# Layer 0 of a two-layer decoder: later places in the code for three loads, another order of the query products, another weave

## The chip, the cores and the metric

The kernel runs on one core of a Trainium2 chip. Its engines are TensorE (PE for its matmuls, PEld for its weight loads), VectorE (DVE), ScalarE (ACT), GpSimd (POOL) and SyncE (SP). SP issues most DMAs and computes nothing; POOL issues DMAs as well as computing. The metric is the device time of one execution in microseconds (us), lower is better; a kernel's time is the median of its runs.

## The reference

Two layers over 1024 tokens of width 1024, in float32. Cut to the part that the change touches, layer 0:

```python
def even_mixer(h, ...):                      # layer 0
    z = h @ w_in                             # qa, ka, va | cq | ckv | kr
    # A: sliding-window attention, 8 heads, window 128, rotary on qa and ka
    # B: latent attention, 8 heads: rms_norm(cq) @ w_uq -> q_nope, q_rope (rotary)
    #    rms_norm(ckv) @ w_ukv -> k_nope, v;  kr -> k_rope (rotary, shared)
    return concat(oa, ob) @ w_out

for layer in (0, 1):
    x = x + mixer[layer](rms_norm(x, mix_norm))
    x = x + memory_cross_attention(rms_norm(x, x_norm), rms_norm(mem, mem_norm), w_q, w_kv, w_o)
    x = x + swiglu(rms_norm(x, ffn_norm), w_gate, w_up, w_down)
return rms_norm(x, final_norm)
```

The memory (`mem`, 256 tokens) doesn't depend on x, so the keys and values that both layers make of it can be computed at any time.

## The kernel before, in words

**Products.** Each float32 operand is split into a high part h (rounded to the type fp32r) and a low part l, and a product is three matmuls: hh, hl, lh. A weight tile of 128 x 1024 comes by a DMA of 512 KB from SP into a raw tile `wr`, ACT copies it to `wh` (L213), and POOL subtracts in four pieces of 256 columns for `wl` (L182 by way of L217).

**Two lines of work.** The 1024 tokens are done in two halves of 512. A *sparse* line (tiles and matmuls named s) runs the attentions, norms and what follows them for one half, and a *dense* line (named d) runs projections for the other half and, later, the feed-forward net. `g_weave` (L297) runs both as generators: a step of the sparse line yields its size n in matmuls of 512 columns, and then the dense line is advanced by n times a ratio; a `Gap(n)` in the sparse line advances the dense line by n of these units. The ratios of the four mixed stretches are R0 to R4 and RA (L44); RA holds for `g_rest(0, 0)`, the last part of the first stretch. Steps of products in `g_rest` count only 0.05 (`DENSE`).

**Order.** The place in the code is a priority. At build time a scheduler puts each engine's instructions into one fixed order from it, out of code order where an operand or a tile isn't ready by its own reckoning. On the chip each engine, and each DMA queue, goes through its list in order and waits at whatever isn't ready. Tiles come from pools with a fixed number of buffers, given out in code order: the dense line has two raw tiles, three weight slots (a slot is a `wh` and a `wl`) and three PSUM banks; the pool of 16 KB tiles (`B16`, by `big`) has six, the pool `A4` four, and the pool of gain vectors `G` has one, which both lines share.

**The dense line of the first stretch** (`dense`, L1769) does, in this order: `proj0_units(0)`, the projections of layer 0 for the first half, with the read of the second half's tokens (`xB`, `squares_unit`) ahead of the last two units; then four key units and four value units of the memory for layer 0 (`memory_units(0)`, m0), with the norm of the second half (`norm_unit`) between the key units; the read of the first half's tokens `xA` (L1776); the load of the rotary tables `tabB` for the second half (L1780 to L1784, four DMAs at L520 that repeat rows for all partitions); the output projection `out_units` for the heads that are done; `proj0_units(1)`; and `memory_units(1)` (m1), the memory for layer 1. In `proj0_units` the last units are the queries `q_nope(0)`, `q_nope(4)` and then `q_rope`; the latent attention of the sparse line starts when all are marked done (`mark("mla", hf)`).

**The sparse line of the first stretch** (`sparse`, L1792): sliding-window attention `g_swa(0)`, latent attention `g_mla(0)`, then `g_rest(0, 0)`: the last part of the output projection, a norm (`x_norm`), the cross-attention to the memory, and a norm (`ffn_norm`). `g_norm_T` (L408) scales a block of 128 tokens on DVE (L420), has PE turn it (L403) and evacuates it by ACT and DVE; it yields a first `Gap` of N1 or N2 (8 and 15) and a `Gap` of 8 after each block. `factors` and `rstd` (L357) make a block's factor by some dozen DVE instructions on one column.

Queries go through DRAM: `q_rope`'s outcome is stored to `qrd` from the POOL queue (`to_rope`), and `g_mla` loads it from there into `qr` (L1396 to L1399).

Of the kernel before, what the change touches and what calls it, by code (L numbers as in the profile page):

```python
# [9 lines left out]
F32 = mybir.dt.float32  # L10
# [8 lines left out]
P = 128  # L19
S = 1024  # L20
D = 1024
# [17 lines left out]
N1, N2 = 8, 15  # L39
# [1 line left out]
START = ((0, 1), (1, 3))  # L41
PSS = 5
NSC = 2
R0, R1, RA, R2, R3, R4 = 2.6, 1.6, 2.3, 1.6, 2.3, 2.1  # L44


def host_constants():
# [61 lines left out]
class Ring:  # L109
# [3 lines left out]
    def next(self):  # L113
        self.i += 1
        return self.items[(self.i - 1) % len(self.items)]
# [47 lines left out]
class Builder:  # L163
# [430 lines left out]
    def memory_units(self, l, s):  # L594
        nc, I = self.nc, self.I
        ma = []

        xn = []

        def load():  # L600
            for b in range(2):
                xn.append(self.A4.tile([P, D], F32, tag="a4", name="mxn"))
                nc.sync.dma_start(xn[b], I["mem"][0, b * P:(b + 1) * P, :])
            return self.gain(f"l{l}_mem_norm")

        def prep(g):
            if l == 0:
                ss = self.st.tile([P, 4], F32, tag="ss", name="ss")
                for i in range(4):
                    nc.scalar.activation(self.t2(), xn[i // 2][:, i % 2 * 512:i % 2 * 512 + 512], AF.Square,  # L610
                                         accum_out=ss[:, i:i + 1])
                nc.vector.tensor_add(ss[:, 0:2], ss.rearrange("p (b h) -> p h b", h=2)[:, 0],
                                     ss.rearrange("p (b h) -> p h b", h=2)[:, 1])
                nc.vector.tensor_copy(self.rmem, self.rstd(ss[:, 0:2], 2, D))
            for b in range(2):
                nc.vector.scalar_tensor_tensor(xn[b], xn[b], self.rmem[:, b:b + 1], g, op0=ALU.mult, op1=ALU.mult)
            return iter(())

        def norm(_):
            m = self.big("mem")  # L620
            mv = [t.rearrange("p (k t) -> p k t", t=MEM) for t in (m[:, 0:2048], m[:, 2048:4096])]
            ma[:] = [(mv[0][:, k], mv[1][:, k]) for k in range(8)]
            for b in range(2):
                yield from self.g_turn(s if l else self.S, xn[b], lambda k0: tuple(t[:, k0:k0 + 4, b * P:(b + 1) * P] for t in mv))

        w = I[f"l{l}_w_xkv"]
        mkv = self.mkv[l]

        def save(ps, c):
            h, lo = self.a4()  # L630
            n = ps.shape[-1]
            self.split_ps(h[:, :n], lo[:, :n], ps)

            def put():
                self.move(mkv[:, c:c + n], h[:, :n])
                self.move(mkv[:, c + 1024:c + 1024 + n], lo[:, :n])

            self.later(put)

        pss = []  # L640

        def key(h):
            def f(wt):
                ps = s.ps()[:, :MEM]
                yield from self.g_projA(ps, wt, ma)
                save(ps, h * MEM)
            return lambda: self.wcols(s, w, h * P), f

        def value(k):
            def f(wt):  # L650
                if k == 0:
                    pss[:] = [s.ps() for _ in range(2)]
                for b in range(2):
                    c = slice(b * P, (b + 1) * P)
                    for j in range(2):
                        ah, al = ma[k + j]
                        for i, (a, x) in enumerate(((ah, wt[0]), (ah, wt[1]), (al, wt[0]))):
                            nc.tensor.matmul(pss[b], a[:, c], x[:, j], start=(k + j + i == 0),
                                             stop=(k + j == 7 and i == 2))
                        yield 3  # L660
                if k == 6:
                    for b in range(2):
                        save(pss[b], 2048 + b * 512)
            return lambda: self.wcols(s, w, 512, 512, k, 2), f

        yield load, prep
        yield (lambda: None), norm
        for h in range(4):
            yield key(h)
        for k in range(0, 8, 2):  # L670
            yield value(k)
        yield self.mark("mem", l)
# [267 lines left out]
    def g_rest(self, l, hf, x, xsrc, out, c0=0):  # L940

        nc, I, st, s = self.nc, self.I, self.st, self.S
        ts = slice(hf * 512, (hf + 1) * 512)
        if x is None:
            x = self.xtile("x")
# [2 lines left out]
                    nc.gpsimd.dma_start(x[tb], xsrc[hf * 512 + tb * P:hf * 512 + (tb + 1) * P, :])  # L948

        after, r = self.factors(x)  # L950

        def out_proj():
            with ExitStack() as es:
                o = self.pool(es, f"op{l}{hf}", 1 if c0 else 2)
                for c in range(c0, 4):
                    h = o.tile([P, 1024], F32R, tag="oh", name="oh")
                    lo = o.tile([P, 1024], F32R, tag="ol", name="ol")
                    with self.hold(HOLD):
                        self.split_in(s, h, lo, [(lambda raw: raw.rearrange("p (k t) -> p k t", t=512),
                                                  self.OTd[c * 256:(c + 1) * 256, ts].rearrange("(k p) t -> p k t", p=P))], "dve", nc.gpsimd)  # L960
                    yield from self.g_accum(s, [(h[:, j * 512:(j + 1) * 512], lo[:, j * 512:(j + 1) * 512])
                                                for j in range(2)], I[f"l{l}_w_out"], c * 256, x, after if c == 3 else None)

        yield from self.scaled(out_proj(), DENSE)
        g = self.gain(f"l{l}_x_norm")
        hx, dst = self.new_acts("hx")
        yield from self.g_norm_T(s, x, g, dst, N1, 8, r)
        after, r = self.factors(x)
        with ExitStack() as es:
            q = self.pool(es, f"xq{l}{hf}", 1).tile([P, 4, 2, 512], F32R, name="xq")  # L970
# [73 lines left out]
                                                    I[f"l{l}_w_xo"], c * 256, x, after if c else None), DENSE)  # L1044
        g = self.gain(f"l{l}_ffn_norm")
        a, dst = self.new_acts("hf")
        yield from self.g_norm_T(s, x, g, dst, N2, 8, r)
        out += [a, x]


    def proj0_units(self, hf, tab, s, given, mem=None, beside=()):
# [3 lines left out]
        nc, I = self.nc, self.I  # L1055
# [131 lines left out]
        f = [None, None]  # L1187
# [31 lines left out]
        def q_nope(h0):  # L1219
            def use(wt):  # L1220
                for pr in range(2):
                    yield from plain(wt, cq, pr * P, self.to_queries(4 + h0 // 2 + pr, hf))
            return (lambda: self.wheads(s, wq[:, :, :, 0:64], slice(h0, h0 + 4), (3, 4, 64))), use
# [47 lines left out]
        yield nq  # L1271
        yield kr_weights, rope_key
        yield sq
        yield q_nope(0)
        yield from others()
        yield q_nope(4)
        yield q_rope_weights, q_rope
        yield self.mark("mla", hf)

    def g_swa(self, hf):  # L1280
# [406 lines left out]
    def body(self, const, x_in, xd):  # L1687
        nc, I = self.nc, self.I
        S_, D_ = self.S, self.D
# [3 lines left out]
        xA = self.xtile("xA")  # L1693
        nc.sync.dma_start(xA[0], x_in[0:P, :])
        g = self.gain("l0_mix_norm")
        nc.sync.dma_start(self.ident, I["c_ident"])
        hA, dst = self.new_acts("hA")
# [27 lines left out]
        hB, xB, xA = [], [], []  # L1725
# [22 lines left out]
        def norm_unit(tb):  # L1748
            def use(_):
                prev = normed.prev  # L1750
                if tb < 4:
                    xn = self.scratch()
                    nc.vector.scalar_tensor_tensor(xn, xB[tb], normed.r[:, tb:tb + 1], normed.g, op0=ALU.mult, op1=ALU.mult)
                    normed.prev = xn
                if tb == 0:
                    h, normed.dst = self.new_acts("hB")
                    hB.append(h)
                else:
                    yield from self.g_turn(D_, prev, lambda k0: normed.dst(k0, tb - 1))

            return none, use

        def until(n):
            def use(_):
                yield Until(lambda: len(self.ots) >= n)

            return [(none, use), (none, lambda _: iter(()))]

        def dense():  # L1769
            m0 = self.memory_units(0, D_)  # L1770
            yield from self.proj0_units(0, tab, D_, [hA], m0, [lambda: (), lambda: (), squares_unit])
            for tb in range(5):
                yield norm_unit(tb)
                if tb < 4:
                    yield next(m0)
            yield (lambda: read(xA, 0)), lambda _: iter(())  # L1776
            yield from m0
            tabB = []

            def load():  # L1780
                tabB.append(self.big("tabB", F32))
                tabs(tabB[0], 1)

            yield load, lambda _: iter(())  # L1784
            yield from until(8)
            yield from self.out_units(0, 0, D_, xA, (0, 1))
            m1 = self.memory_units(1, D_)
            yield from self.proj0_units(1, tabB[0], D_, hB, None, [
                lambda: until(12) + self.out_units(0, 0, D_, xA, (2,)) + [self.mark("out", 0)]])
            yield from m1  # L1790
# [11 lines left out]
        fA, xA = nxt  # L1802
# [28 lines left out]
        fA, xA = nxt  # L1831
# [49 lines left out]
```

## Time and profile before

| | |
|---|---|
| median of 3 runs | 2963.68 us (2961.78 to 2965.33) |
| the profiled execution, whole | 2964.39 us |
| its span, first to last instruction | 2962.6 us |
| PE busy | 2801.5 us (95%) |
| POOL, DVE, ACT busy | 1752.9 us (59%), 1653.8 us (56%), 1308.3 us (44%) |
| DMA | 416.67 MB, 141 GB/s over the span |

An engine's busy time is the union of its instructions; a wait is idle time ahead of an instruction, with what ended it. In the page's slices PE stands at 7 to 9 tenths up to about 300 us and again around 550 us, and at 9 almost everywhere else. PEclk is the clock that TensorE was granted, as a share of 2.4 GHz; its other level is 1.2 GHz, 0.5. The first mixed stretch ends at about 570 us, where the feed-forward net of the first half begins; all that the change touches by name lies before that, except that `proj0_units` and `memory_units` serve both halves and both layers of that stretch.

### The profile page before, as it was taken

How to read it: one execution, taken by the hardware profiler on the slowest of the kernel's cores; microseconds unless marked ns; L12 is line 12 of the kernel's file. 1: busy time of each engine (PE TensorE's matmuls, PEld its weight loads, DVE VectorE, ACT ScalarE, POOL GpSimd, SP SyncE). 2: the span in 40 equal slices, each digit the busy share in tenths (PEclk: the TensorE clock that was granted, in tenths of full speed). 3: DMA queues.
4: the chain of work that ended last, by engine and by line, in shares of the span. 5: the costliest groups of instructions: out<-in, count | busy, mean ns of one | idle time of the engine just before them, and what ended most of it. 6: DMA issues, size and time to landing. Idle time of an engine off the chain costs nothing. (4 is left out here: it accounts for less than half of the span.)

```text
span 2962.6 us, 39653 instructions
## 1 busy us (share of the span) xinstructions
PE 2801.5 (95%) x13524; PEld 2332.7 (79%) x13524; DVE 1653.8 (56%) x3665; ACT 1308.3 (44%) x2543; POOL 1752.9 (59%) x2471
## 2 busy tenths in 40 slices
PE   7777989699999999999999999999999999999998
PEld 6656777588888888887888887877887888788887
DVE  6675567356665556256665646245777645642223
ACT  5644445354443343265444343356565433422222
POOL 3676646685554465666666465566776755555553
PEclk9979999899999999999999999999999999999999
DMA  5566443644434333554545333465545533233331
GB/s 174 160 203 217 150 157 99 192 131 136 138 124 129 122 92 128 154 190 154 155 151 174 107 101 121 140 201 178 168 146 166 174 107 114 93 121 100 93 100 64
DMA packets 385078, 416.67 MB, mean 141 GB/s; under 512 B 32940, under 2 KB 295340, under 8 KB 384876
## 3 DMA queue, kind: packets, MB, share of 16 engines
q1 hardware_dynamic: 333980, 248.30, 28.4%
q0 software_dynamic: 50896, 165.85, 16.8%
q8 instruction: 107, 1.75, 0.2%
q14 instruction: 95, 0.78, 0.1%
HBM read 346.04 MB, written 68.03 MB: 140 GB/s over the span
## 5 line engine op out<-in xcount | busy, mean ns | idle before, releaser
L182 POOL TENSOR_TENSOR wl<-wr,wh 128x256 fp32r<-128x256 f32 (+1 forms) x1692 | 1236.5, 767 | 787.1 <-ACT wh L213 706.8
L213 ACT ACTIVATE wh<-wr 128x1024 fp32r<-128x1024 f32 (+1 forms) x421 | 443.0, 1056 | 761.4 <-PE d L240 401.3
L240 PE MATMUL d<-hfh,wh 128*128 128x512 f32 x1408 | 559.7, 398 | 8.0 <-ACT wh L213 6.3
L240 PE MATMUL d<-hfh,wl 128*128 128x512 f32 x1408 | 554.8, 394 | 0.0
L240 PE MATMUL d<-hfl,wh 128*128 128x512 f32 x1408 | 552.5, 392 | 0.0
L240 PE MATMUL d<-wh,a 128*128 128x512 f32 x1440 | 521.3, 396 | 11.2 <-DVE x L690 4.1
L690 DVE TENSOR_TENSOR x<-d,x 128x512 f32<-128x512 f32 x344 | 234.9, 687 | 360.9 <-PE d L240 359.3
L240 PEld LDWEIGHTS d<-wh,a 128*128 128x128 f32 x1440 | 270.5, 188 | 68.7 <-DVE x L690 5.8
L240 PEld LDWEIGHTS d<-hfh,wh 128*128 128x128 f32 x1408 | 265.9, 189 | 56.8 <-ACT wh L213 7.3
L240 PEld LDWEIGHTS d<-hfh,wl 128*128 128x128 f32 x1408 | 265.2, 188 | 51.8
L240 PEld LDWEIGHTS d<-hfl,wh 128*128 128x128 f32 x1408 | 265.5, 189 | 48.8
L240 PE MATMUL d<-wl,a 128*128 128x512 f32 x720 | 282.2, 392 | 0.1
L690 DVE TENSOR_TENSOR x<-s,x 128x512 f32<-128x512 f32 x168 | 112.8, 687 | 98.7 <-PE s L240 98.1
L240 PEld LDWEIGHTS d<-wl,a 128*128 128x128 f32 x720 | 135.6, 188 | 25.0 <-POOL wl L182 0.4
L791 ACT ACTIVATE af<-af,nm 128x512 f32<-128x512 f32 (+3 forms) x160 | 93.9, 588 | 110.5 <-DVE nm L787 109.0
L185 ACT ACTIVATE ph<-s 128x512 fp32r<-128x512 f32 (+1 forms) x158 | 85.0, 552 | 113.7 <-PE s L814 105.5
L182 DVE TENSOR_TENSOR pl<-s,ph 128x512 fp32r<-128x512 f32 (+1 forms) x158 | 98.6, 632 | 64.9 <-ACT ph L185 64.2
L240 PE MATMUL s<-hmh,wl 128*128 128x512 f32 x256 | 100.4, 392 | 3.0 <-POOL wl L182 3.0
L787 DVE CUSTOM_DVE_ANT_0 af<-s,bias 128x512 f32<-128x512 f32 (+3 forms) x128 | 67.6, 536 | 60.2 <-PE s L778 44.6
L240 PE MATMUL s<-hmh,wh 128*128 128x512 f32 x256 | 99.9, 390 | 0.1
L182 DVE TENSOR_TENSOR a<-d,a 128x512 fp32r<-128x512 f32 (+2 forms) x105 | 68.4, 652 | 56.5 <-ACT a L185 55.1
L240 PE MATMUL s<-hml,wh 128*128 128x512 f32 x256 | 99.7, 389 | 0.0
(370 smaller groups left out, 5662.4 us busy)
## 6 DMA issues: line engine op xcount, KB each, us to landing
wr<-in_l_w_gate SPq DMA_DIRECT2D x88, 512.0 KB, 4.8
wr<-in_l_w_up SPq DMA_DIRECT2D x88, 512.0 KB, 3.9
wr<-in_l_w_down SPq DMA_DIRECT2D x88, 512.0 KB, 3.6
wr<-in_l_w_qkv SPq DMA_DIRECT2D x48, 512.0 KB, 3.9
wr<-in_l_w_out SPq DMA_DIRECT2D x32, 512.0 KB, 3.8
tab<-qd POOLq DMA_DIRECT2D x32, 512.0 KB, 5.8
ar<-qd POOLq DMA_DIRECT2D x24, 512.0 KB, 7.0
wr<-in_l_w_in SPq DMA_DIRECT2D x22, 512.0 KB, 4.7
```

What stands on the lines that cost most here:

```text
L182: e.tensor_sub(out, x, h.bitcast(F32))
L185: self.nc.scalar.activation(h, ps, AF.Copy)
L213: self.nc.scalar.activation(h, raw[:, :n], AF.Copy)
L240: self.nc.tensor.matmul(ps, a, b, start=(3 * i + j == 0), stop=(3 * i + j == n - 1))
L690: self.nc.vector.tensor_add(xs, ps, xs)
L787: nc.vector.tensor_tensor_reduce(p[:, c:c + n], t, bias[:, b0 + c:b0 + c + n], -scale, lim, ALU.add, ALU.min, accum_out=nm)
L791: nc.scalar.activation(p[:, c:c + n], p[:, c:c + n], AF.Exp, bias=nm, scale=-1.0, accum_out=l[:, i:i + 1])
```

## The change

- In `dense`, a key unit of m0 now comes ahead of each `norm_unit`, and the first two value units stand before and after the last one; the read of `xA` comes after them; and the load of `tabB` comes after the output projection of the heads 0 to 7 instead of before it.
- In `memory_units(1)` the two memory blocks and the gain go into weight slots of the dense line (two blocks into one slot's `wh` and `wl`, the gain into another's `wh`) and no longer into two `A4` tiles and the `G` tile. For layer 0 the tiles are the same as before.
- In `proj0_units`, for both halves, `q_rope` comes before `q_nope(0)` and `q_nope(4)`.
- RA goes from 2.3 to 1.7; in `g_rest(0, 0)` alone the gaps of both norms become 24 at the start and 14 after each block.

```diff
-R0, R1, RA, R2, R3, R4 = 2.6, 1.6, 2.3, 1.6, 2.3, 2.1
+R0, R1, RA, R2, R3, R4 = 2.6, 1.6, 1.7, 1.6, 2.3, 2.1
...
         def load():
+            if l == 0:
+                xn[:] = [self.A4.tile([P, D], F32, tag="a4", name="mxn") for _ in range(2)]
+                g = self.G.tile([P, D], F32, tag="g", name="g")
+            else:
+                xn[:] = [t.bitcast(F32) for t in s.slot()]
+                g = s.slot()[0].bitcast(F32)
             for b in range(2):
-                xn.append(self.A4.tile([P, D], F32, tag="a4", name="mxn"))
                 nc.sync.dma_start(xn[b], I["mem"][0, b * P:(b + 1) * P, :])
-            return self.gain(f"l{l}_mem_norm")
+            src = I[f"l{l}_mem_norm"]
+            nc.sync.dma_start(g, bass.AP(tensor=src.tensor, offset=src.offset, ap=[[0, P], [1, D]]))
+            return g
...
         after, r = self.factors(x)
+        n1, n2, gap = (24, 24, 14) if l + hf == 0 else (N1, N2, 8)
...
-        yield from self.g_norm_T(s, x, g, dst, N1, 8, r)
+        yield from self.g_norm_T(s, x, g, dst, n1, gap, r)
...
-        yield from self.g_norm_T(s, x, g, dst, N2, 8, r)
+        yield from self.g_norm_T(s, x, g, dst, n2, gap, r)
...
         yield sq
+        yield q_rope_weights, q_rope
         yield q_nope(0)
         yield from others()
         yield q_nope(4)
-        yield q_rope_weights, q_rope
         yield self.mark("mla", hf)
...
-            for tb in range(5):
+            for tb in range(4):
+                yield next(m0)
                 yield norm_unit(tb)
-                if tb < 4:
-                    yield next(m0)
+            yield next(m0)
+            yield norm_unit(4)
+            yield next(m0)
             yield (lambda: read(xA, 0)), lambda _: iter(())
             yield from m0
+            yield from until(8)
+            yield from self.out_units(0, 0, D_, xA, (0, 1))
             tabB = []
...
             yield load, lambda _: iter(())
-            yield from until(8)
-            yield from self.out_units(0, 0, D_, xA, (0, 1))
```

## Rows read from the trace of the kernel before

**Rows 1.** Busy time by stretch: length, busy us (instructions) per engine, clock, DMA share, GB/s.
```profile
130.00:600.00 470.00, 383.74 (x1876) 315.16 (x1874) 280.12 (x653) 219.14 (x451) 289.90 (x413) 0.91 0.54 166
600.00:2962.60 2362.60, 2318.00 (x11160) 1933.79 (x11160) 1289.89 (x2823) 1019.04 (x1956) 1393.69 (x1963) 1.00 0.43 134
```

**Rows 2.** The same view of five shorter stretches (PE, PEld, DVE, ACT, POOL).
```profile
505.00:533.00 28.00, 13.91 (x68) 11.11 (x66) 26.74 (x63) 13.28 (x22) 13.97 (x21) 0.75 0.57 194
541.00:569.00 28.00, 24.75 (x146) 20.68 (x145) 3.09 (x7) 8.44 (x13) 19.00 (x30) 0.97 0.40 121
...
384.00:405.00 21.00, 14.37 (x62) 10.61 (x63) 19.16 (x48) 11.44 (x20) 7.69 (x8) 0.84 0.31 87
169.00:219.00 50.00, 29.46 (x129) 24.27 (x128) 33.03 (x54) 20.77 (x37) 38.16 (x58) 0.73 0.67 211
435.00:482.00 47.00, 45.76 (x233) 37.33 (x232) 29.71 (x61) 24.46 (x60) 36.40 (x45) 1.00 0.44 126
```

**Rows 3.** Timeline of PE: start, length, instruction, count, idle before and releaser.
```profile
199.28 0.80 PE L240 MATMUL d<-mem,wh 128*128 128x256 f32 x2 [7.09 <-DVE a L182]
...
212.08 0.77 PE L778 MATMUL s<-KR,qr 128*128 128x128 f32 x2 [5.72 <-DMA qr<-qrd]
...
272.99 0.58 PE L825 MATMUL s<-ph,ar 128*128 128x256 f32 x1 [13.73 <-ACT ph L185]
```

**Rows 4.** Timeline of SP's queue: start, time to the last issue, DMA, count.
```profile
220.60 0.66 SPq L351 DMA_DIRECT2D g<-in_l_x_norm  x1
...
250.43 3.62 SPq L520 DMA_DIRECT2D tabB<-tabs  x4
254.22 3.83 SPq L211 DMA_DIRECT2D wr<-in_l_w_out  x1
```

**Rows 5.** DMA issues between 250 and 275 us: count, KB each, us to landing.
```profile
tabB<-tabs SPq DMA_DIRECT2D x4, 256.0 KB
...
wr<-in_l_w_out SPq DMA_DIRECT2D x1, 512.0 KB, 17.2
```

**Rows 6.** DMA issues of the whole execution, the page's part 6.
```profile
wr<-in_l_w_out SPq DMA_DIRECT2D x32, 512.0 KB, 3.8
```

**Rows 7.** Timeline of POOL, its DMA issues for the rotary queries.
```profile
199.19 0.63 POOL L178 DMA_DIRECT2D qrd<-a  x1 [0.81 <-DVE a L182]
...
206.81 2.97 POOL L178 DMA_DIRECT2D qr<-qrd  x6
```

**Rows 8.** PE groups, 197 to 205 us: count, busy us, mean ns, idle before.
```profile
L240 PE MATMUL d<-mem,wl 128*128 128x256 f32 x8 | 3.3, 415 | 0.0
```

**Rows 9.** PE groups, 542.8 to 549 us, the same products.
```profile
L240 PE MATMUL d<-mem,wh 128*128 128x256 f32 x36 | 6.7, 289 | 0.0
L240 PE MATMUL d<-mem,wl 128*128 128x256 f32 x17 | 4.8, 283 | 0.0
```

**Rows 10.** Timeline of DVE: a rotary multiply, and one column of a factor.
```profile
190.80 0.68 DVE L533 TENSOR_TENSOR t<-d,tab 128x512 f32<-128x512 f32 x1
...
511.44 3.19 DVE L364 SCALAR_TENSOR_TENSOR ra<-rr 128x1 f32<-128x1 f32 x1
514.56 0.15 DVE L364 SCALAR_TENSOR_TENSOR ra<-rg 128x1 f32<-128x1 f32 x1
```

**Rows 11.** Timeline of POOL at the same time, a split of one weight tile.
```profile
511.79 2.82 POOL L182 TENSOR_TENSOR wl<-wr,wh 128x256 fp32r<-128x256 f32 x4
```

**Rows 12.** Timeline of PE in the second norm.
```profile
517.57 1.09 PE L403 MATMUL s<-ident,xn 128*128 128x128 f32 x8 [3.66 <-DVE xn L420]
527.03 1.97 PE L403 MATMUL s<-ident,xn 128*128 128x128 f32 x8 [8.37 <-DVE xn L420]
...
537.68 3.68 PE L403 MATMUL d<-ident,mxn 128*128 128x128 f32 x16 [6.36 <-DVE mxn L616]
```

**Rows 13.** Timeline of SP's queue in the second norm.
```profile
523.20 0.90 SPq L603 DMA_DIRECT2D mxn<-in_mem  x2
529.26 0.33 SPq L351 DMA_DIRECT2D g<-in_l_mem_norm  x1
```

## The prediction

> **What bounds the kernel now.** I read the busy time by stretch first. Behind 600 us PE is busy 2318.0 of 2362.6 us at full clock, so little is to be had there; between 130 and 600 us, all of it the first mixed stretch, it is busy 383.7 of 470 us at a mean clock of 0.91 [rows 1]. The change can be worth at most those 86 us of idle time and what the lower clock costs. TensorE's work itself stays the same, so a gain is idle time removed. I then read the five shorter stretches, and in each what PE waited for. Three kinds of stall stand out. (a) From 259.3 to 273.0 us nothing runs: PE waits 13.73 us for `ph` [rows 3], ACT's queue being held by the copy of a `w_out` tile that took 17.2 us to land [rows 5], where this DMA's median is 3.8 [rows 6]. In SP's queue it stands right behind the four DMAs of `tabB`, 1 MB [rows 4, 5]. (b) Around the start of the latent attention, 169 to 219 us, PE is busy 29.5 of 50 us at a clock of 0.73 [rows 2]. (c) At the two norms, 384 to 405 us and 505 to 541 us, PE waits for DVE: in the second norm 3.66 + 8.37 + 6.36 = 18.4 us [rows 12].
>
> A low clock adds to each stall. Eight of the 256-column matmuls at 199 us took 415 ns each, behind 7.09 us of idle time [rows 3, 8]; the same form at 543 us took 283 ns, 53 of them in 6.2 us, so 0.117 us apart [rows 9]. A matmul of 512 columns, the unit of the weave, is thus 0.23 us.
>
> **The change part by part.**
>
> *Tables later* (a). Nothing is removed; the 1 MB moves behind four units of the output projection in code order. If `w_out` no longer queues behind it, 13.7 us go. But one thing tells against a sure gain: code order is only a priority. The gain of `x_norm` was issued at 220.60 us [rows 4], though the norm that uses it runs after 384 us [rows 2]: the scheduler issues a load when its tile comes free, wherever it stands in the code. The order in which `big` hands out tiles is the same before and after (`xB`, two for the attention, two for `hB`, `xA`, `tabB`), and `tabB` takes the tile of the memory activations, free at the same point of the dense line. What the move can do is let `w_out` win where both are ready. It may, since it was issued only 3.8 us after `tabB` [rows 4]. Behind `tabB` would then stand the operand of the second pair of heads, needed two units (48 x 0.23 = 11 us) later. Bounds 0 and 14; I take 10, nearer the upper one, since the burst is also spread by the rest of the change.
>
> *Tokens later.* The same: the read of `xA` takes `xB`'s tile when it is free. Nothing is queued behind it that the trace shows as late; I cost it at 0, and if the cover is gone it costs its issue, under 3 us.
>
> *Rotary queries first, memory keys before the norm blocks* (b). `q_rope`'s stores left POOL last, at 199.19 us, so the loads of `qr` went out at 206.81 [rows 7] and the first scores waited 5.72 us until 212.08 [rows 3]. With two units of `q_nope`, 36 x 0.23 = 8.3 us, behind it, the stores leave that much earlier, and this wait is gone; next late is `KR`, or the plain queries. The other wait, 7.09 us [rows 3], is the dense line out of PSUM banks while DVE is late; a key unit ahead of each norm block puts products of 24 half-size matmuls there instead, and rotary's longer chain on DVE (multiply, multiply, add, subtract: 4 x 0.68 us against 2 x 0.68 for a plain pair [rows 10]) no longer ends the run. It costs the same chain some 10 us earlier, beside the window attention: two blocks x 2 extra x 0.68, with the two table multiplies 4 us on DVE, of which none to all may show. `q_nope(4)`'s weights now stand behind `xB` in SP's queue where `q_rope`'s stood; both are three DMAs. Bounds: -4, and the two waits with 3 us of clock, 16. I take 8, half, because DVE and DMA stay loaded there (33.0 of 50 us, share 0.67 [rows 2]).
>
> *Weave* (c). By counting yields: `g_rest(0, 0)` owed the dense line 8 + 4 x (4 x 2.3 + 8) = 77 units in its first norm and 84 in its second, now 24 + 4 x (4 x 1.7 + 14) = 107 in each; 64 x 2.3 = 147 in the cross-attention, now 64 x 1.7 = 109; with the rest 347, now 356. The dense line has 411 left at that point, so both leave about 60 units alone at the end: the balance holds, and 38 units (8.7 us) go from the cross-attention to the norms. In the first norm PE idled 21.0 - 14.4 = 6.6 us while DVE was busy 19.2 [rows 2]. The products cover PE, but DVE sets when the norm ends: bounds -3 and 6, I take 2. In the cross-attention PE was busy 45.8 of 47 us [rows 2]; with 8.7 us less cover 0 to 8 us show. I take 3.
>
> *Second memory in weight slots* (c). Before, its gain waited for the one `G` buffer and went out at 529.26, six us after the memory itself [rows 13]; the turns began at 537.68 [rows 12], and then 24.8 us of products ran alone [rows 2], right behind 28 us in which PE did 13.9 us [rows 2]. Now the blocks go out when `q_rope`'s slot is free and the gain when `q_nope(0)`'s is, both before the second norm's middle. The products can fill the 18.4 us, and the lower clock there (0.75 [rows 2]) adds about 5. Against it: two of three slots are held, so the first key's weights wait for the last query unit and come some 8 us behind it (3.8 to land [rows 6], ACT, 2.8 on POOL [rows 11]), hidden in part by the turns. Bounds 5 and 23; I take 14.
>
> Sum: 10 + 0 + 8 + 2 - 3 + 14 = 31 us. From the profiled execution's 2964.4 (span 2962.6 and 1.8 around it; 0.7 over the median) that is **2933 us**. The bounds together reach from 10 us slower to 59 faster.
>
> One row speaks against more products beside a norm. A DVE instruction on one column took 3.19 us where the next took 0.15 [rows 10], and POOL was splitting a weight tile for 2.82 us of that time [rows 11]. The Trainium skill has a rule for it: GPSIMD Engine Reference, section "Specifications", says that POOL's SBUF interfaces are shared with VectorE, with contention for instructions that have two SBUF inputs. The row agrees; the rival below takes it as the bound.
>
> **The rivals.**
>
> *The tables stay where they are in the queue.* For it: the row of the `x_norm` gain. Against it: near ties are settled by priority, and the key units shift what is ready. The stall of (a) remains and the rest comes: 2964 - 21 = 2943.
>
> *VectorE takes the norms' gain back.* In the second norm DVE is busy 26.7 of 28 us [rows 2]. If four more tiles are split beside its chain at 2.8 us each, up to 11 us of what the second memory frees are spent in DVE's queue, the first norm and the cross-attention end even, and (b) comes in half: 14 - 11 + 4 + a third of (a) = 10, so 2954. It decides if the splits meet the factor chain, as one did [rows 10, 11]. The skill's rule would give this by itself.
>
> *The dense line starves* (slower). Two held slots leave one for weights, so two key units run at 3.8 + 1.1 + 2.8 = 7.7 us each in place of 2.8: 10 us; the cross-attention shows its 8; (a) stays and (b) gives 8. 2964 + 10 = 2974. It decides from the point where the gains of (a) and (b) are under 18.
>
> *Nothing of it.* The scheduler undoes the moves, and the weave only trades one zone for another: 2961.
>
> **How the numbers follow.** Forecast 0.48, from 2918 to 2940; tables 0.20, 2943; VectorE 0.14, 2954; starved 0.10, 2974; nothing 0.08, 2961. A difference of 0.2%, 6 us, is about what a measurement of this kernel can tell from none. Faster by more: 0.48 + 0.20 + 0.13 = 0.81. Within: 0.01 + 0.08 + 0.01 = 0.10. Slower: 0.09. The range leaves out the starved case and the far end of the bounds (59 us faster): 2908 to 2962.
>
> **What would show it.** Right: no wait over 5 us at the first `ph` behind `tabB`, and a `w_out` there landing in under 6 us; the `qr` loads before 200 us and no wait for them; the gain of the second memory out before the second norm's last block, and `mem` products between its turns; the first feed-forward product some 30 us earlier than 569 us. Wrong: `tabB` still directly ahead of a `w_out` in SP's queue; a new wait of the key units for `wh`; idle PE in the cross-attention above 5 us; or a change of more than 5 us behind the first stretch, where I cost nothing.

## The result and the profile after

The changed kernel takes 2948.16 us (median, 2945.21 to 2953.59) against 2963.68 for the kernel before: a ratio of 0.9949, 95% interval [0.9934, 0.9964]. It is 15.5 us faster, half of the 31 that the prediction forecast; the sign is right, the size is not. The profiled execution took 2948.16 us too, with a span of 2946.4.

The first mixed stretch now ends at 547 us (the first feed-forward product), not at 569: 22 us were won there, and 5.5 of them were given back behind it. First the kernel before, then the changed one:

```profile
569.12 0.40 PE L240 MATMUL d<-hfh,wh 128*128 128x512 f32 x1
```

```profile
547.44 0.39 PE L240 MATMUL d<-hfh,wh 128*128 128x512 f32 x1
```

Five views say where. The first is TensorE's timeline around the latent attention, with idle time and releaser in brackets; it answers [rows 3].

```profile
196.84 0.50 PE L240 MATMUL d<-mem,wh 128*128 128x256 f32 x2 [3.69 <-DVE a L182]
202.18 1.22 PE L785 MATMUL s<-ar 128*128 128x128 f32 x4 [3.19 <-DMA ar<-qd]
...
234.77 0.33 PE L821 MATMUL s<-ident,af 128*128 128x128 f32 x1 [3.38 <-DVE af L803]
...
278.69 0.45 PE L821 MATMUL s<-ident,af 128*128 128x128 f32 x1 [12.38 <-DVE af L803]
```

The wait of 5.72 us for the rotary queries is gone, and 3.19 for the plain ones stands in its place. The wait of 7.09 us is 3.69. The stall of 13.73 us is still there, with 12.38 us, under another name. The second view, ACT's and SP's timelines at that place, answers [rows 4].

```profile
250.34 0.37 SPq L211 DMA_DIRECT2D wr<-in_l_w_out  x1
260.81 1.83 SPq L520 DMA_DIRECT2D tabB<-tabs  x3
262.75 0.72 SPq L211 DMA_DIRECT2D wr<-in_l_w_out  x1
263.52 0.74 SPq L520 DMA_DIRECT2D tabB<-tabs  x1
...
276.58 1.06 ACT L213 ACTIVATE wh<-wr 128x1024 fp32r<-128x1024 f32 x1 [12.19 <-DMA wr<-in_l_w_out]
...
277.54 0.39 ACT L798 ACTIVATE af<-af,nm 128x128 f32<-128x128 f32 x1
```

Three of the four DMAs of `tabB` still stand ahead of the second `w_out` tile. Of SP's waits between 235 and 300 us (us in total, times, longest) this one held them:

```profile
SPq L520 <- PE d L665: 10.0, 1, 10.0
```

So SP stood 10.0 us at `tabB`, whose tile the last value product of the memory (L665) had to free, with `w_out` queued behind it. `w_out` then landed beside the tables, so late that its copy began 13.8 us after its issue at 262.75, and ACT, which takes its list in order, held its copy and with it the attention's exponentials (L798), the scaling on DVE (L803) and PE's turns (L821). It is [rows 4, 5] over again.

The third view is the second norm, PE's and SP's rows, answering [rows 12, 13].

```profile
495.19 0.34 SPq L608 DMA_DIRECT2D wh<-in_mem  x1
495.64 0.36 SPq L608 DMA_DIRECT2D wl<-in_mem  x1
499.27 0.33 SPq L610 DMA_DIRECT2D wh<-in_l_mem_norm  x1
...
505.84 0.66 PE L403 MATMUL d<-ident,wh 128*128 128x128 f32 x4 [0.53 <-DVE wh L623]
509.25 1.12 PE L403 MATMUL d<-ident,wh 128*128 128x128 f32 x4 [2.75 <-DVE t L1139]
...
515.24 1.16 PE L240 MATMUL d<-mem,wh 128*128 128x256 f32 x2 [2.35 <-DVE ra L364]
520.76 1.03 PE L403 MATMUL s<-ident,xn 128*128 128x128 f32 x8
```

The second memory and its gain go out as the norm begins (its first turn is at 499.31), its products lie between the norm's turns (`s<-ident,xn`), and the waits of 3.66, 8.37 and 6.36 us are now 2.75 and 2.35. The fourth view is the busy time by stretch, cut at the same points of the work: second norm to the first feed-forward product, and from there some 510 us on. Columns: length, busy us (instructions) of PE, PEld, DVE, ACT, POOL, clock, DMA share, GB/s. First the kernel before, then the changed one.

```profile
511.00:569.00 58.00, 35.98 (x201) 30.03 (x200) 27.69 (x50) 20.49 (x32) 31.54 (x49) 0.79 0.59 183
569.00:1078.00 509.00, 497.48 (x2520) 416.51 (x2519) 295.51 (x657) 225.89 (x470) 293.52 (x418) 1.00 0.43 131
```

```profile
499.00:547.00 48.00, 37.48 (x212) 30.93 (x211) 26.24 (x52) 19.92 (x30) 34.68 (x51) 0.89 0.68 208
547.00:1059.00 512.00, 498.53 (x2518) 418.52 (x2517) 304.69 (x657) 227.54 (x470) 295.70 (x419) 0.99 0.42 129
```

The first stretch is 10 us shorter, the second 3 us longer. The fifth view is a sum over the trace: TensorE's lost time by stage, that is its idle time plus half of the time that it was busy at the lower of its two clock levels. The stages are cut at landmarks of the work: the first value product of the first memory, the first product on `hB`, the first turn of each norm, the first product on `hx`, the first feed-forward product and the 900th; a wait counts to the stage that begins with the instruction behind it, and the last stage ends with TensorE's last product. A difference of the sums agrees with that of the spans to 3 us. Losses in us, one profile each, so small differences say little (no_dense and tables_moved, whose queues have the same order at the tables, are 4.4 apart in the second stage):

```
                    before  after  rotary  dense  slots  weave  tables_  no_     tables_
                                   _only   _only  _only  _only  alone    dense   moved
0-130                 35.1   36.2   34.9   35.0   36.8   34.9   35.1     34.3    36.6
130-first value       36.6   26.0   28.3   31.8   33.7   35.3   35.5     25.2    29.6
 -first hB            26.8   30.5   24.0   30.5   29.2   28.5   12.8     23.0    21.6
 -first norm           1.3    0.4    0.7    0.9    0.9    1.1    1.3      0.7     0.7
 -first hx             7.3    2.4    1.9    1.6    7.5    5.8    6.9      2.3     2.3
 -second norm          3.4    2.4    0.8    0.6    3.4    5.1    5.4      2.4     2.4
 -first feed-forward  26.5   14.0   22.1   26.6   20.2   28.3   25.6     16.1    16.1
 -900th               13.0   18.4   16.1   13.4   16.5   12.4   19.9     15.2    13.9
 -end                 36.1   38.1   36.7   34.6   35.9   36.3   37.6     36.8    37.3
sum                  186.1  168.4  165.5  175.0  184.1  187.7  180.1    156.0   160.5
```

By stage, the changed kernel wins 10.6 us up to the first value product, loses 3.7 in the stage of the tables, wins 0.9 ahead of the first norm, 4.9 in it, 1.0 in the cross-attention and 12.5 at the second norm, and loses 5.4 and 2.0 behind that and 1.1 at the start: 17.7 us in all, of a span that is 16.2 us shorter. The tables, forecast to give 10, gave nothing: their stage loses 3.7 more. That and the 7.4 behind the first stretch (5.5 by the span), costed at nothing, are more than the whole shortfall of 15.5.

### The profile page after: what moved, and what is told of

Same layout as the page of the kernel before. It is cut to its first block, busy times and chain, and to the rows that moved or that the text cites. A ratio compares the mean times of both kernels' runs of the same rounds, so it can differ in the third digit from the quotient of the medians.

```text
span 2946.4 us, 39628 instructions
## 1 busy us (share of the span) xinstructions
PE 2807.2 (95%) x13524; PEld 2335.4 (79%) x13524; DVE 1670.9 (57%) x3665; ACT 1309.2 (44%) x2543; POOL 1761.4 (60%) x2471
## 5 line engine op out<-in xcount | busy, mean ns | idle before, releaser
L182 POOL TENSOR_TENSOR wl<-wr,wh 128x256 fp32r<-128x256 f32 x1692 | 1245.1, 772 | 766.5 <-ACT wh L213 687.9
L213 ACT ACTIVATE wh<-wr 128x1024 fp32r<-128x1024 f32 x421 | 442.9, 1056 | 778.7 <-PE d L240 416.7
L240 PE MATMUL d<-hfh,wh 128*128 128x512 f32 x1408 | 560.7, 398 | 10.6 <-ACT wh L213 5.9
L798 ACT ACTIVATE af<-af,nm 128x512 f32<-128x512 f32 (+3 forms) x160 | 93.9, 588 | 87.0 <-DVE nm L794 85.7
L728 DVE SCALAR_TENSOR_TENSOR d<-t,d 128x512 f32<-128x512 f32 x88 | 60.8, 691 | 62.4 <-PE d L240 61.9
L724 DVE SCALAR_TENSOR_TENSOR t<-t,d 128x512 f32<-128x512 f32 x88 | 60.0, 682 | 63.5 <-ACT t L723 62.7
```

Of the source, the lines that this page charges most:

```text
L182: e.tensor_sub(out, x, h.bitcast(F32))
L213: self.nc.scalar.activation(h, raw[:, :n], AF.Copy)
L240: self.nc.tensor.matmul(ps, a, b, start=(3 * i + j == 0), stop=(3 * i + j == n - 1))
L724: nc.vector.scalar_tensor_tensor(t, t, 1.0, pg, op0=ALU.add, op1=ALU.mult)
L728: nc.vector.scalar_tensor_tensor(pu, t, 0.5, pu, op0=ALU.mult, op1=ALU.mult)
L798: nc.scalar.activation(p[:, c:c + n], p[:, c:c + n], AF.Exp, bias=nm, scale=-1.0, accum_out=l[:, i:i + 1])
```

## The experiments

Each kernel is compared with the kernel before on the same chip; times are medians, with the ratio's 95% interval. The first four ask whether the tables' place in the queue is the step that failed, and what each part does alone.

**tables_behind**: the changed kernel with the four DMAs of `tabB` bound in SP's queue behind the last `w_out` tile of the heads 0 to 7.

```diff
-            (queue or self.nc.sync).dma_start(at(raw), src)
+            d = (queue or self.nc.sync).dma_start(at(raw), src)
+            if s is self.D:
+                self.last = d
...
-                tabs(tabB[0], 1)
+                with self.tc.issue_after(self.last.ins):
+                    tabs(tabB[0], 1)
```

> The changed kernel, with the four table DMAs of the second half bound in SP's queue behind the last weight tile of the output projection for heads 0 to 7. Theory: the stall of 12.4 us at 266 us in the changed kernel is a w_out tile that queues behind three of the four table DMAs; with the tables really moved, that tile lands in under 7 us, the stall shrinks to under 3 us, and the time falls by 9 to 14 us against the changed kernel (to about 2937). Rival 1: the tile is late by the stores of the memory's values and the head loads of the same moment, which stay: it still takes over 12 us, and nothing is gained. Rival 2: the tables' 1 MB now holds up the w_in tile behind it, a new stall of 5 us or more at about 305 us, and half of the gain is given back.

Measured: 2940.99 us, 0.9926 [0.9913, 0.9938], 7 us under the changed kernel, where 9 to 14 were expected. The wait of 12.38 us is down to 3.00:

```profile
269.71 0.84 PE L823 MATMUL s<-ident,af 128*128 128x128 f32 x3 [3.00 <-DVE rl L804]
```

The stall is the tables' doing. But 2941 is still 8 us over the forecast, so it isn't all of the shortfall.

**dense_only**: the kernel before with the last part of the change alone, the new order in `dense` (the last three pieces of the diff shown, L1776 to L1786 of the kernel before).

> The kernel before, with the new order of the dense line alone (key units ahead of the norm blocks, tokens and tables later in the code). Theory: code order is a priority only, so SP's queue keeps the tables directly ahead of the second w_out tile, and the 13.7 us stall stays within 2 us; the key units ahead give 0 to 5 us of the idle time between 169 and 219 us. Time 2958 to 2965. Rival: the later place in the code takes the tables out of the way in this kernel, and the stall goes: 2950 or less.

Measured: 2953.02 us, 0.9968 [0.9957, 0.9979]: 10 us faster, more than expected. The order of SP's queue around the tables is that of the kernel before (one `w_out`, four `tabB`, the second `w_out`), so the later place in the code moved nothing there. The wait, though, didn't stay within 2 us of 13.7 as expected: the longest behind the tables is 5.43 us, while 9.27 us, for the copy of a value weight, now stand ahead of them, and the stage loses 30.5 us against 26.8.

```profile
238.64 1.22 PE L658 MATMUL d<-wh,mem 128*128 128x512 f32 x2 [9.27 <-ACT wh L213]
282.48 1.22 PE L240 MATMUL d<-wh 128*128 128x512 f32 x2 [5.43 <-ACT wh L213]
```

The gain lies elsewhere: 5.7 us at the first norm and 4.8 up to the first value product.

**rotary_only**: the kernel before with `q_rope` ahead of `q_nope(0)`, and nothing else.

```diff
         yield sq
+        yield q_rope_weights, q_rope
         yield q_nope(0)
         yield from others()
         yield q_nope(4)
-        yield q_rope_weights, q_rope
```

> The kernel before, with the rotary queries first and nothing else. Theory: the wait of 5.7 us for the rotary queries at the first scores of the latent attention is gone and the products start there 5 to 10 us earlier; 4 to 10 us gained, 2954 to 2960. Rival: the wait is replaced by one for the plain queries or the shared key part, and the gain is under 2 us.

Measured: 2938.04 us, 0.9915 [0.9899, 0.993]. This one edit alone beats the whole change by 10 us, and gives far more than the 4 to 10 expected. SP's queue shows a part of why:

```profile
251.53 3.12 SPq L211 DMA_DIRECT2D wr<-in_l_w_out  x2
263.19 3.62 SPq L520 DMA_DIRECT2D tabB<-tabs  x4
```

Both `w_out` tiles now go ahead of the tables, although the load of `tabB` is where it was in the code. PE's wait at the tables is 4.44 us:

```profile
274.57 0.48 PE L827 MATMUL s<-pl,ar 128*128 128x128 f32 x1 [4.44 <-DVE pl L182]
```

The stage of the tables loses 24.0 us here, against 30.5 in the changed kernel; against the 26.8 of the kernel before that is only 2.8 won. The rest is 8.3 us up to the first value product, 8.6 from the first product on `hB` to the second norm, and 4.4 at that norm.

**slots_only**: the kernel before with the second memory in weight slots alone (the `load` of `memory_units`).

> The kernel before, with the memory of layer 1 in weight slots and nothing else. Theory: the memory's turns and products move between the turns of the second norm, idle time of PE between 505 us and the feed-forward net falls from 22 to 8 to 14 us, and the time by 8 to 14 us, 2950 to 2956. Rival: without the wider gaps of the norm the dense line has used up its products before the norm ends and its weights starve on the one slot left, so the gain is under 5 us.

Measured: 2958.97 us, 0.9986 [0.9977, 0.9995]. The second norm's stage loses 20.2 us in place of 26.5, and 3.5 of the 6.3 come back in the feed-forward stage. Alone, this part is worth a third of what the forecast gave it.

So the parts alone give 10, 25 and 4 us, and with the weave together 15.5: they work against one another. The next four ask which.

**no_dense**: the whole change without the new order in `dense`.

> The whole change without the new order of the dense line: rotary queries first, second memory in weight slots, the weave. In the built order of SP's queue the two w_out tiles stand ahead of the four DMAs of tabB, as in rotary_only; in the changed kernel three of the four stand ahead of the second w_out. Theory (the new dense order turns that near tie back, and so brings the stall at the tables back into the change): the wait of 12.4 us near 266 us is under 5, and the time is about 10 us under the changed kernel's, 2932 to 2940. Rival (the parts gain the same microseconds, so that rotary first has no more to give once the others are there): 2945 to 2950, whatever stands in the queue.

Measured: 2936.34 us, 0.991 [0.9896, 0.9923], 12 us under the changed kernel. The queue and the wait are as in rotary_only:

```profile
247.55 3.12 SPq L211 DMA_DIRECT2D wr<-in_l_w_out  x2
259.20 2.53 SPq L520 DMA_DIRECT2D tabB<-tabs  x4
...
270.27 0.47 PE L834 MATMUL s<-pl,ar 128*128 128x128 f32 x1 [4.11 <-DVE pl L182]
```

The new dense order, worth 10 us by itself, costs 12 where the rotary queries are first.

**no_weave**: the changed kernel with RA back at 2.3 and the gaps of both norms at 8 or 15 and 8.

> The changed kernel with the old weave (RA 2.3, gaps of 8 or 15 and 8). Its SP queue has the tables ahead of the second w_out as the changed kernel has. Theory (the weave fills the norms): the stretch of the second norm and the second memory up to the first feed-forward product, 14 us of lost TensorE time in the changed kernel, has about 20 as in slots_only, and the time is 4 to 8 us over the changed kernel's, 2952 to 2956. Rival (the products beside the norms are paid for behind the first stretch, where the changed kernel lost 7.7 us more than the kernel before): that loss is gone too, and the time is 2944 to 2950.

Measured: 2945.57 us, 0.9943 [0.9929, 0.9956], no slower than the changed kernel. Neither theory's mechanism holds: the second norm's stage loses 13.4 us with the old weave and 14.0 with the new one, and the feed-forward stage 19.1 against 18.4. The weave does nothing clear of the noise here, so it isn't what fills the second norm.

**weave_only**: the kernel before with RA at 1.7 and the gaps of 24 and 14.

> The kernel before with the weave alone: RA 1.7, and gaps of 24 and 14 in both norms of the first half's rest. The forecast's step: the first norm gives 2, the cross-attention costs 3, so 2963 to 2967. Rival (the products cover the second norm too, even with the second memory's gain late): the second norm's waits of 18.4 us fall by 4 to 8, and the time is 2955 to 2960.

Measured: 2963.91 us, 1.0003 [0.9993, 1.0012]. The forecast's step holds: the first norm gains 1.5 us, the cross-attention loses 1.7. The second norm's stage gains nothing (28.3 us lost against 26.5), so the rival falls.

**rot_slots_tables**: the kernel before with rotary first, the second memory in weight slots, and `tabB` loaded behind the output projection of the heads 0 to 7 and bound there as in tables_behind.

> The kernel before with rotary queries first, the second memory in weight slots, and the four DMAs of tabB bound in SP's queue behind the last w_out tile of the heads 0 to 7; the dense line's order else and the weave stay as before. Theory (three separate stalls): rotary_only's 2938 less 4 to 6 for the second memory, as slots_only gave, less up to 4 for what was left of the stall at the tables: 2928 to 2934, faster than the changed kernel and than each part alone. Rival (what is gained ahead of the feed-forward net is lost behind it, as with slots_only): 2935 to 2940.

Measured: 2934.73 us, 0.9904 [0.989, 0.9917], just over the theory's upper end, and faster than the changed kernel by 13 us. Over rotary_only's 2938 the second memory and the bound tables add 3 us, which the two intervals don't tell from nothing.

The last four cut the dense order in two, and price the stall by itself.

**tables_moved**: the whole change, but of the new dense order only the load of `tabB` behind the output projection; norm blocks, keys and the tokens' read as before.

```diff
-            for tb in range(4):
-                yield next(m0)
-                yield norm_unit(tb)
-            yield next(m0)
-            yield norm_unit(4)
-            yield next(m0)
+            for tb in range(5):
+                yield norm_unit(tb)
+                if tb < 4:
+                    yield next(m0)
```

> The whole change but with the old order of norm blocks and keys and of the tokens' read: of the dense line's new order only the load of tabB keeps its later place in the code. The built order of SP's queue has both w_out tiles ahead of tabB, as no_dense. Theory (the key units ahead of the norm blocks turn the near tie back; the tables' place in the code does nothing): the same as no_dense, 2932 to 2940, and no wait over 5 us between 255 and 285 us. Rival (it is the later place of the tables that costs): 2944 to 2950.

Measured: 2933.04 us, 0.9895 [0.9882, 0.9909], and the fastest kernel here beside rot_slots_tables. That it is the forecast's number is luck: by stage it wins 7.0 us up to the first value product, 5.2 at the tables, 5.0 in the first norm and 10.4 at the second, where the forecast had 8, 10, 2 and 14.

```profile
253.54 3.12 SPq L211 DMA_DIRECT2D wr<-in_l_w_out  x2
265.19 2.74 SPq L520 DMA_DIRECT2D tabB<-tabs  x4
...
276.37 0.47 PE L834 MATMUL s<-pl,ar 128*128 128x128 f32 x1 [4.23 <-DVE pl L182]
```

**tables_unmoved**: the changed kernel with the load of `tabB` back ahead of the output projection; key units stay ahead of the norm blocks.

> The changed kernel with the load of tabB at its old place in the code; the key units stay ahead of the norm blocks. In the built order all four DMAs of tabB stand ahead of the second w_out (three of four in the changed kernel). Theory: the stall of 12 us stays, and the time is the changed kernel's or up to 4 us more, 2946 to 2953. Rival (the tables' place costs): 2934 to 2942.

Measured: 2950.2 us, 0.9952 [0.9937, 0.9968], as the theory had it. All four DMAs of `tabB` stand ahead of the second `w_out`, and the wait is 14.55 us:

```profile
260.34 2.72 SPq L520 DMA_DIRECT2D tabB<-tabs  x4
263.18 0.67 SPq L211 DMA_DIRECT2D wr<-in_l_w_out  x1
...
280.39 0.45 PE L821 MATMUL s<-ident,af 128*128 128x128 f32 x1 [14.55 <-DVE af L803]
```

These two settle it. The place of the tables' load in the code is worth 2 us (tables_unmoved against the changed kernel) or 3 (no_dense against tables_moved), neither clear of the noise; the key units ahead of the norm blocks, with the read of the tokens that moved with them, cost 15 us where the rotary queries are first.

**tables_alone**: the kernel before with `tabB` bound behind the last `w_out` of the heads 0 to 7, and nothing else.

> The kernel before with one thing changed: the four DMAs of tabB bound in SP's queue behind the last w_out of the heads 0 to 7, which the two loads' place in the code alone did not bring about. It prices the stall that the forecast put at 10 (0 to 14). Theory: the wait of 13.7 us for ph goes to under 4 and the time falls by 7 to 12, to 2951 to 2956. Rival (what waits for the tables, or the next wait of the latent attention, takes its place): 2957 to 2963.

Measured: 2954.93 us, 0.997 [0.996, 0.998], 9.5 us faster. The longest wait between 230 and 330 us is 2.05 us, and the stage of the tables loses 12.8 us in place of 26.8. The first feed-forward product comes 14.1 us earlier, at 555.0 us, but the profiled execution ends only 8.7 us earlier: 5.4 us are given back behind the first stretch, 3.8 of them in the feed-forward stage.

**rot_slots_weave_tables**: rot_slots_tables with the weave added.

> Rotary queries first, the second memory in weight slots, the weave, and tabB bound in SP's queue behind the last w_out of the heads 0 to 7; the order of norm blocks and keys as before. Against rot_slots_tables it adds the weave alone. Theory (the weave trades one zone for another and is worth nothing here, as weave_only and no_weave say): within 3 us of rot_slots_tables, 2932 to 2938. Rival (with the second memory early, more products beside the norm pay): 2926 to 2931.

Measured: 2940.25 us, 0.9924 [0.9912, 0.9937]: outside both, 5.5 us slower than rot_slots_tables. The two intervals meet, so a cost of the weave here is likely and not shown. Its stage of the tables loses 27.2 us against 23.5, the second norm's 17.7 against 15.1, and the feed-forward stage 15.8 against 15.2, but the profile of rot_slots_tables is its fastest run (2928.25). Why stays open.

## Why the prediction was right and wrong

**Tables later: the step that failed.** The forecast took 10 us for it, on the reason that `w_out` might win where both loads are ready. It weighed the right row against that, the `x_norm` gain issued long ahead of its use, and then set it aside; the rival "the tables stay where they are in the queue" describes what happened, though its 2943 is 5 us off. Alone, the dense order left that part of SP's queue as it was; in the changed kernel the tables' place in the code let one of four DMAs slip behind `w_out`: 2 us by tables_unmoved, within the noise. The price of the stall was right: bound behind `w_out`, the tables give 9.5 us in tables_alone, against the 10 forecast. What failed is the belief that moving the call moves the load.

**What decided instead** was a part that the forecast had the other way round: "the key units shift what is ready" stands there as a reason for the tables to move out of the way. Rotary first, alone, puts both `w_out` tiles ahead of the tables; key units ahead of the norm blocks, on top of it, put three of the four table DMAs back. Six kernels show the pair. With both `w_out` ahead (rotary_only, no_dense, tables_moved) the wait there is 4.44, 4.11 and 4.23 us and the time 2933 to 2938; with tables between them (after, no_weave, tables_unmoved) it is 12.38, 12.24 and 14.55 and the time 2946 to 2950. The kernel before, weave_only and slots_only have the tables between them too, with waits of 13.73, 11.63 and 12.89; dense_only is the exception, with 5.43, so the order alone doesn't fix the wait. Why the scheduler orders them so wasn't shown; each order is fixed when the kernel is built.

The stall is not the whole of that difference: tables_behind, where it is gone, stays at 2941, 8 us over tables_moved. In their profiled executions, 5.6 us apart, both reach the first feed-forward product at 541 us; 3.9 of the 5.6 lie in the feed-forward stage (18.3 us lost against 13.9), which is where the changed kernel loses too.

**Rotary first and keys ahead (b): right.** Forecast 8, measured 10.6 in its stage. The stores leave POOL early and the loads of `qr` go out from 194.00 us, not 206.81 [rows 7]:

```profile
184.59 0.65 POOL L178 DMA_DIRECT2D qrd<-tab  x1 [2.41 <-PE d L240]
194.00 0.54 POOL L178 DMA_DIRECT2D qr<-qrd  x1
```

Next late are the plain queries, 3.19 us, as the prediction said. Only its credit was shared wrongly: the keys aren't needed for it (rotary_only wins 8.3 us there, no_dense 11.4, tables_moved 7.0).

**Weave (c).** For the first norm 2 was forecast and 4.9 measured, but not by the weave: rotary_only and dense_only lose 1.9 and 1.6 us there without it, weave_only still 5.8. In the kernel before, the dense line's own norm (`d<-t,ones`, waiting for DVE) fell in the middle of the sparse line's:

```profile
387.74 1.09 PE L403 MATMUL s<-ident,xn 128*128 128x128 f32 x8 [2.38 <-DVE xn L420]
390.63 2.08 PE L1104 MATMUL d<-t,ones 128*128 128x512 f32 x2 [1.80 <-DVE t L1096]
398.32 0.60 PE L403 MATMUL s<-ident,xn 128*128 128x128 f32 x4
```

In the changed kernel it comes behind all but the last two turns of the sparse one:

```profile
385.16 0.87 PE L403 MATMUL s<-ident,xn 128*128 128x128 f32 x6 [1.56 <-DVE xn L420]
386.83 1.13 PE L1112 MATMUL d<-t,ones 128*128 128x512 f32 x2 [0.80 <-DVE t L1104]
391.93 0.38 PE L403 MATMUL s<-ident,xn 128*128 128x128 f32 x2
```

The loss goes with that place throughout the table: 5.8 to 7.5 us where the dense norm lies in the middle (before, slots_only, weave_only, tables_alone), 1.6 to 2.4 where it lies at the end (about 4 in no_weave and tables_behind, which the table leaves out). That this shift is the cause is argued from the rows, not tried by itself. The cross-attention, forecast to lose 3, lost nothing. The 1.0 won there is the wait ahead of its first product, 1.15 us in the kernel before, which ends the norm; the idle time is nowhere near the 5 us that the prediction named as a sign of being wrong.

**Second memory in weight slots (c): the size is right, the credit isn't shown.** Forecast 14, measured 12.5 at the second norm, with the memory's products between the norm's turns as forecast. But slots_only shows 6.3 there and rotary_only, without the slots, 4.4, and no run leaves the slots alone out of the change.

**Behind the first stretch: costed at 0, measured 7.4 (5.5 by the span).** Of the 5.4 us that the feed-forward stage loses more, 2.0 are idle time (13.5 us against 11.5) and 3.4 the lower clock. Both kernels wait over 5 us at its start, for the copy of a weight, and the granted clock fell to 1.2 GHz around that wait in both, but for 10 us in the changed kernel and for 3 in the kernel before (a mean clock of 0.50 and 0.83 over 10 us; columns as above, the kernel before first):

```profile
580.36 0.72 PE L240 MATMUL d<-hfh,wh 128*128 128x512 f32 x1 [5.17 <-ACT wh L213]
...
580.00:590.00 10.00, 7.95 (x34) 6.26 (x35) 5.72 (x23) 5.38 (x20) 5.99 (x8) 0.83 1.06 286
```

```profile
558.84 0.80 PE L240 MATMUL d<-hfh,wh 128*128 128x512 f32 x1 [5.34 <-ACT wh L213]
...
557.00:567.00 10.00, 6.46 (x22) 5.31 (x23) 4.77 (x19) 4.97 (x16) 4.75 (x7) 0.50 1.04 266
```

The feed-forward stage loses 12.4 to 13.4 us in before, weave_only and dense_only, and 18.3 to 19.9 in after, no_weave, tables_unmoved, tables_behind and tables_alone. It goes neither with the weave nor with one part of the change; what sets it stays open.

**The rivals.** "VectorE takes the gain back" falls: the second norm gave 12.5. What it rests on is there all the same, and small:

```profile
511.64 1.58 DVE L366 SCALAR_TENSOR_TENSOR rg<-ra,rr 128x1 f32<-128x1 f32 x1
513.75 0.15 DVE L366 SCALAR_TENSOR_TENSOR rr<-ra,rg 128x1 f32<-128x1 f32 x1
...
510.42 2.77 POOL L182 TENSOR_TENSOR wl<-wr,wh 128x256 fp32r<-128x256 f32 x4
```

An instruction on one column took 1.58 us while POOL split a tile, and one of the same line took 0.15 after it. The rule of the Trainium skill that the prediction cited (GPSIMD Engine Reference, "Specifications") agrees with these rows. The instruction was 1.4 us longer beside POOL, and what that cost in time isn't shown. "The dense line starves" falls as well: the longest wait for a key or value weight at the end of the stretch is 1.61 us (`wh`, at 543.52). "Nothing of it" falls with the ratio. One sum of the prediction is off: its bound of 10 us slower leaves out the 3 us that it allowed for the tokens; nothing hangs on it.

## What to carry to other kernels

Where a build-time scheduler orders the queues, moving a load in the code need not move it in the queue; read the built order of the queue, and if the order matters, bind the load behind the one it must not hold up. Two edits that each help can undo one another through the order of one queue, so time each alone and the whole with each left out. When a stall is removed early in a long kernel, part of it can be lost again later: tables_alone was 14.1 us ahead at the first feed-forward product and 8.7 at the end.

## What the runs showed of the hardware

A stall is longer than its idle time, since the clock falls with it. The changed kernel's stretches around the 12.38 us show it (columns as above):

```profile
246.00:266.00 20.00, 17.82 (x94) 13.67 (x92) 10.41 (x30) 10.51 (x21) 16.33 (x28) 1.00 0.59 173
266.00:279.00 13.00, 0.62 (x3) 0.18 (x1) 0.87 (x4) 1.93 (x5) 1.68 (x3) 0.66 0.60 188
279.00:290.00 11.00, 10.25 (x42) 8.71 (x42) 8.24 (x28) 5.67 (x16) 6.30 (x12) 0.63 0.54 180
290.00:300.00 10.00, 10.00 (x47) 8.14 (x46) 6.23 (x10) 2.31 (x4) 3.31 (x5) 1.00 0.13 31
```

PE was idle in nearly all of 266 to 279 us, and then worked 11 us at a mean clock of 0.63, about 8 of them at 1.2 GHz; by 290 it was back at 2.4 GHz. At half speed those 8 us are an estimated 4 us more. One engine's in-order list carries a late load far: the `w_out` tile belongs to the dense line, and through ACT's one copy it stopped the attention of the sparse line on ACT, DVE and PE.
